# Two landing blocks of the experts' loads become places for split weights

## The chip, the cores and the metric

The kernel runs on one core of a Trainium2 chip. The metric is the time of one execution on the device in microseconds (us): the median of three runs.

The core has TensorE for matrix products (its matmul stream is PE in the profile, its weight loads PEld), VectorE (DVE), ScalarE (ACT), GpSimd (POOL) and SyncE (SP), whose queue issues the DMA transfers that bring the weights from device memory. Each engine works through its own instructions in order, and semaphores make an engine wait for another.

## The reference

Two layers on 256 tokens of width 1024, all in 32-bit floats. Each layer is a mixer (attention beside a gated delta rule) and a feed-forward part; the feed-forward part of the second layer is a mixture of eight experts. The change touches that part alone. Without the sorting of tokens into blocks it computes:

```python
logits = xt @ router_w + router_b                # 256 tokens x 8 experts
top_val, top_idx = lax.top_k(logits, 2)
gates = jax.nn.softmax(top_val, axis=-1)
# for each expert e and the tokens x that chose it:
gt, up = jnp.split(x @ w_gate_up[e], 2, axis=-1) # 1024 x 7168
y = (jax.nn.silu(gt) * up) @ w_down[e]           # 3584 x 1024
out[token] += gate * y
```

All eight experts are used, so all their weights (8 x 42 MB) are read once.

## The kernel before

**Splitting.** TensorE multiplies in a reduced form of 32-bit floats. To keep the accuracy each operand is taken as a high part (its rounding to that form) and a low part (the rest), and a product is the sum of three: high x high, low x high, high x low. Weights land unsplit: `load` issues a transfer of 1 MB (a unit: 128 partitions x 2048 floats) into a landing block, named raw. ScalarE rounds the unit to its high part (`wh_e`, L1058), and VectorE subtracts this from the landed unit and gets the low part (`wl_e`, L1071). When the subtraction is done, the landing block is free for another load. When TensorE is done with the unit's matmuls, the places of both parts are free.

**Blocks.** `ring` (L1507) lists the landing blocks in the order in which loads take them: seven of the eight blocks c0 to c7 that the mixer used before, and five (`NRAW`) of a pool of their own, twelve in all. Block c7 is one of three places for low parts. There are four places for high parts; only unit 0 has its high part elsewhere, in c6, so the load that takes c6 has to wait until TensorE has used unit 0.

**Order of the work.** The experts' part has 336 units. `sources` lists them: for each chunk of 512 of an expert's 3584 inner columns four units of gate and up weights, and then the two down units of the chunk before. Experts are ranked by their number of tokens. The first runs alone, then come three pairs of a full expert (up to 128 tokens) and a half one (up to 64), chunk by chunk in turn, and the last runs alone. A unit costs TensorE 12 matmuls of 512 columns for a full expert and 8 for a half one (there high and low parts of the tokens stand side by side in one operand).

`unit` calls `Weights.take(i)` ahead of the matmuls of unit i. It first sees to it that all units up to a distance ahead are cast (`hi`) and subtracted (`lo`). `pin` keeps these instructions, and the matmuls, in program order on their engines, so the two distances in `take` fix how far ScalarE and VectorE stand ahead of TensorE:

```python
self.hi(i + 4)
self.lo(i + 3)
return self.his[i], self.los[i]
```

A chunk then goes: product pg (`gu`, two units), ScalarE's SiLU of it (egt), product pu (two units), VectorE's product of both for a full expert, the down part of the chunk before (`finish`, two units, out py or pya and pyb), and the turn of the result: transposes pet for a full expert, with its split on ScalarE and VectorE (eah, eal), and products with a folding matrix, pef, for a half one (then esg and ea). Before the second chunk of the first expert stands `gates`, some 33 small VectorE instructions that work out the gates and the ranks of the experts. The rows of the experts' tokens are gathered and their results added by indirect DMAs from GpSimd (`gather`, `add_rows`).

A planner puts instructions that aren't pinned, the loads on SyncE among them, into an order of its own.

Of the kernel before, what the change touches and what calls it, by code (L numbers as in the profile page):

```python
# [12 lines left out]
F32R = mybir.dt.float32r  # L13
# [5 lines left out]
P = 128  # L19
# [5 lines left out]
NRAW = 5  # L25
# [4 lines left out]
UNIT = 2048  # L30
# [65 lines left out]
def build(ctx, tc, nc, A, out, upto=99):  # L96
# [75 lines left out]
    def block(tag, name, shape=(P, UNIT), dtype=F32):  # L172

        return cb.tile(list(shape), dtype, tag=tag, name=name)

    ring, nraw, halves = [None] * NRAW, [0], [2]

    def load(src):
        tag = ring[nraw[0] % len(ring)]
        nraw[0] += 1  # L180
        name = f"raw{nraw[0]}"
        if tag is None:
            raw = rawp.tile([P, UNIT], F32, tag="raw", name=name)
        else:
            raw = block(tag, name)
        n = UNIT // halves[0]
        for i in range(halves[0]):
            nc.sync.dma_start(raw[:, i * n:(i + 1) * n], src[:, i * n:(i + 1) * n])
        halves[0] = 1
        return raw  # L190
# [843 lines left out]
    def moe(l, ep, wp, dram):  # L1034
# [3 lines left out]
        def pin(ins):  # L1038

            return tc.keep_in_program_order(ins)  # L1040

        class Weights:
# [6 lines left out]
            def hi(self, n):  # L1049
                while len(self.his) < min(n, len(self.srcs)):  # L1050
                    i = len(self.his)
                    raw = load(source(*self.srcs[i]))
                    if self.ahead and i == 0:
                        h = block("c6", f"wh_{self.name}{i}", dtype=F32R)
                        SC.copy(h, raw)
                    else:
                        h = wp.tile([P, UNIT], F32R, tag="wh", bufs=4, name=f"wh_{self.name}{i}")
                        pin(SC.copy(h, raw))  # L1058
                    self.raws.append(raw)
                    self.his.append(h)  # L1060

            def lo(self, n):
                while len(self.los) < min(n, len(self.srcs)):
                    i = len(self.los)
                    self.hi(i + 1)
                    raw, h = self.raws[i], self.his[i]
                    if i % 3 == 0:
                        w = block("c7", f"wl_{self.name}{i}", dtype=F32R)
                    else:
                        w = wp.tile([P, UNIT], F32R, tag="wl", bufs=2, name=f"wl_{self.name}{i}")  # L1070
                    ins = V.tensor_tensor(w, raw, h, op=ALU.subtract)  # L1071
                    if i or not self.ahead:
                        pin(ins)
                    self.los.append(w)

            def take(self, i):

                self.hi(i + 4)
                self.lo(i + 3)
                return self.his[i], self.los[i]  # L1080


# [3 lines left out]
        def source(name, q, u):  # L1086
            if number[q] is None:
                number[q] = nc.values_load(who[0:1, q:q + 1], engines=[mybir.EngineType.SP], min_val=0, max_val=E - 1)
            return A[name][number[q], u]
# [413 lines left out]
    if upto >= 4:  # L1503
        with tc.tile_pool(name="wp", bufs=1) as wp, tc.tile_pool(name="over", bufs=1) as over, tc.tile_pool(name="ep", bufs=1) as ep, \
                tc.tile_pool(name="es", bufs=1) as es, \
                tc.tile_pool(name="dram", bufs=1, space=bass.MemoryType.DRAM) as dram:
            ring[:] = ["c3", "c1", "c2", "c0", "c4", "c5", "c6"] + [None] * NRAW  # L1507
            nraw[0] = 0

            over.tile([P, 384], F32, name="over")  # L1510
            moe(1, Even(ep, es), wp, dram)
# [6 lines left out]
def program(arrays, upto=99):  # L1518
    nc = bacc.Bacc("TRN2", target_bir_lowering=False, num_devices=1)
    A = {k: nc.dram_tensor(k, a.shape, mybir.dt.from_np(a.dtype), kind="ExternalInput").ap() for k, a in arrays.items()}  # L1520
    out = nc.dram_tensor("out", (1, S, D), F32, kind="ExternalOutput").ap()
    with tile.TileContext(nc, schedule_with_timeline_sim=True) as tc, ExitStack() as ctx:
        build(ctx, tc, nc, A, out, upto)
    return nc
# [46 lines left out]
```

## Time and profile before

| | us |
|---|---|
| median of three runs | 1581.25 (1579.4 to 1581.94) |
| the profiled execution | 1583.06 |
| its span, first to last instruction | 1581.3 |
| first matmul of the experts | 666.6 |
| PE busy, whole span | 1545.1 (98%) |
| PEld busy | 1330.3 (84%) |
| DVE busy | 1340.4 (85%) |
| ACT busy | 1072.6 (68%) |
| 336 subtractions for wl_e on DVE | 754.0, 2.286 each |
| 335 casts for wh_e on ACT | 634.1, 1.915 each |

The profile is of one execution. A busy share is the time in which an engine had an instruction under way; matmuls are pipelined and their ends are modelled, so PE's share says little on how many matmuls fit. Back to back, instructions overlap by about a tenth of a microsecond in the records, so the distance between starts counts. In a row of a timeline the first number is the start, the second the duration, and brackets hold the idle time of the engine ahead of the instruction and what ended it. "Waited for" is the instruction whose end released the waiting one.

### The profile page before, as it was taken

What the parts mean: (1) busy time and instruction counts of PE and PEld (TensorE: products, weight loads), DVE (VectorE), ACT (ScalarE), POOL (GpSimd) and SP (SyncE); (2) the same over time, 40 slices, a digit from 0 to 9 for tenths busy, and PEclk for the clock granted to TensorE, in tenths of its full rate; (3) what the DMA queues carried; (4) which work ended last, traced back from release to release, by engine and by line L of the source; (5) the groups of instructions that cost most, each with busy time, mean ns of one, the idle gap of its engine ahead of it and who ended that gap; (6) DMA issues with size and microseconds to landing.
All of it is one profiled execution on the core that took longest, in us unless ns stands there. A gap on an engine that the chain in (4) does not pass through costs nothing.

```text
span 1581.3 us, 23677 instructions
## 1 busy us (share of the span) xinstructions
PE 1545.1 (98%) x8946; PEld 1330.3 (84%) x8946; DVE 1340.4 (85%) x1511; ACT 1072.6 (68%) x1168; POOL 113.8 (7%) x76
## 2 busy tenths in 40 slices
PE   8999999999999999989999999999999999999997
PEld 6899999999888999878878878877877888888886
DVE  6998776655689977688889999999989999999986
ACT  6655555444575655567768887887878888878773
POOL 0420000000023010100001000010000100000100
PEclk9999999999999999999999999999999999999999
DMA  7433455555543376489999999999999999999980
GB/s 301 160 105 110 156 179 191 191 191 193 169 159 107 108 267 214 165 323 364 368 348 407 421 398 423 393 412 426 426 407 411 396 425 426 426 419 399 412 359 29
DMA packets 67514, 465.84 MB, mean 295 GB/s; under 512 B 8192, under 2 KB 8704, under 8 KB 12608
## 3 DMA queue, kind: packets, MB, share of 16 engines
q1 hardware_dynamic: 64080, 453.95, 73.2%
q0 software_dynamic: 2016, 7.08, 1.7%
q10 hardware_dynamic: 1296, 3.22, 0.6%
q8 instruction: 72, 1.18, 0.3%
q14 instruction: 50, 0.41, 0.1%
HBM read 457.41 MB, written 6.82 MB: 294 GB/s over the span
## 4 chain that ended last, share of the span: by engine, by line
PE 88%; DVE 7%; DMA 1%; ACT 1%; issue 1%; POOL 0%; DVEq 0%; ACTq 0%; SPq 0%
PE pg L1307 16%; PE pu L1307 15%; PE py L1307 12%; PE pf L333 8%; PE pd L333 4%; DVE wl_e L1071 3%; PE p_ga L333 3%; PE p_gb L333 3%; PE p_wo L333 3%; PE pef L1445 2%; PE pyb L1307 2%; PE pya L1307 2%; PE p_z L333 1%; PE p_cq L333 1%; PE p_yb L333 1%; PE p_ya L333 1%
## 5 line engine op out<-in xcount | busy, mean ns | idle before, releaser
L1071 DVE TENSOR_TENSOR wl_e<-raw,wh_e 128x2048 fp32r<-128x2048 f32 x336 | 754.0, 2286 | 10.6 <-ACT wh_e L1058 6.2
L1058 ACT CAST wh_e<-raw 128x2048 fp32r<-128x2048 f32 x335 | 634.1, 1915 | 79.3 <-PE pu L1307 24.2
L1307 PE MATMUL pg<-wh_e,hTe 128*128 128x512 f32 x728 | 250.4, 399 | 0.0
L1307 PE MATMUL pu<-wh_e,hTe 128*128 128x512 f32 x728 | 245.9, 393 | 0.0
L1307 PE MATMUL pu<-wl_e,hTe 128*128 128x512 f32 x448 | 179.9, 401 | 8.6 <-DVE wl_e L1071 7.2
L1307 PE MATMUL pg<-wl_e,hTe 128*128 128x512 f32 x448 | 176.5, 394 | 1.3 <-DVE wl_e L1071 1.3
L1307 PEld LDWEIGHTS pu<-wh_e,hTe 128*128 128x128 f32 x728 | 137.9, 189 | 27.9
L1307 PEld LDWEIGHTS pg<-wh_e,hTe 128*128 128x128 f32 x728 | 137.2, 189 | 27.2
L333 PE MATMUL pf<-hh_ffn,wh_fg 128*128 128x256 f32 x704 | 125.0, 281 | 0.0
L1307 PEld LDWEIGHTS pu<-wl_e,hTe 128*128 128x128 f32 x448 | 84.8, 189 | 38.2 <-DVE wl_e L1071 21.2
L1307 PE MATMUL py<-wl_e,eah 128*128 128x512 f32 x280 | 111.3, 398 | 2.1 <-DVE wl_e L1071 1.0
L1307 PE MATMUL py<-wh_e,eah 128*128 128x512 f32 x280 | 109.7, 392 | 0.7 <-ACT eah L1462 0.7
L1307 PE MATMUL py<-wh_e,eal 128*128 128x512 f32 x280 | 109.5, 391 | 0.0
L333 PEld LDWEIGHTS pf<-hh_ffn,wh_fg 128*128 128x128 f32 x704 | 108.2, 188 | 0.8
L1307 PEld LDWEIGHTS pg<-wl_e,hTe 128*128 128x128 f32 x448 | 84.6, 189 | 18.1 <-DVE wl_e L1071 1.7
L333 PE MATMUL pf<-hh_ffn,wl_fg 128*128 128x256 f32 x352 | 99.0, 282 | 0.0
L168 ACT CAST wh_fg<-raw 128x1024 fp32r<-128x1024 f32 x44 | 46.1, 1049 | 63.8 <-PE pf L333 37.5
L169 DVE TENSOR_TENSOR wl_fg<-raw,wh_fg 128x1024 fp32r<-128x1024 f32 x44 | 53.8, 1225 | 41.1 <-ACT wh_fg L168 41.0
L1307 PEld LDWEIGHTS py<-wl_e,eah 128*128 128x128 f32 x280 | 52.6, 188 | 20.2 <-DVE wl_e L1071 9.8
L333 PEld LDWEIGHTS pf<-hh_ffn,wl_fg 128*128 128x128 f32 x352 | 67.5, 192 | 0.0
L1307 PEld LDWEIGHTS py<-wh_e,eah 128*128 128x128 f32 x280 | 52.6, 188 | 12.7 <-ACT eah L1462 0.9
L1307 PEld LDWEIGHTS py<-wh_e,eal 128*128 128x128 f32 x280 | 52.6, 188 | 10.8 <-DVE eal L1463 0.4
(450 smaller groups left out, 3104.0 us busy)
## 6 DMA issues: line engine op xcount, KB each, us to landing
raw<-moe_w_gate_up SPq DMA_DIRECT2D x224, 1024.0 KB, 8.4
raw<-moe_w_down SPq DMA_DIRECT2D x112, 1024.0 KB, 8.6
raw<-w_in SPq DMA_DIRECT2D x43, 1024.0 KB, 4.8
raw<-ffn_w_gate_up SPq DMA_DIRECT2D x22, 1024.0 KB, 4.8
raw<-ffn_w_down SPq DMA_DIRECT2D x11, 1024.0 KB, 4.7
raw<-w_out SPq DMA_DIRECT2D x8, 1024.0 KB, 4.8
raw<-w_branch_b SPq DMA_DIRECT2D x4, 1024.0 KB, 5.0
raw<-w_branch_a SPq DMA_DIRECT2D x4, 1024.0 KB, 5.3
```

Source lines behind the costliest of these rows:

```text
L168: SC.copy(h[:, q], raw_ap[:, q])
L169: V.tensor_tensor(lo[:, q], raw_ap[:, q], h[:, q], op=ALU.subtract)
L333: T.matmul(o, lhsT, rhs, start=start, stop=stop)
L1058: pin(SC.copy(h, raw))
L1071: ins = V.tensor_tensor(w, raw, h, op=ALU.subtract)
L1307: pin(T.matmul(o, lhsT, rhs, start=start, stop=stop))
L1445: pin(T.matmul(pt_[:, i, t, :], r[:, t * P:(t + 1) * P], halves2, start=i + t == 0, stop=i + t == 4))
```

## The change

`ring` loses c4 and c5: ten landing blocks instead of twelve, and c6 moves from the seventh to the fifth place. c4 becomes a fifth place for high parts (of every fifth unit), c5 a fourth place for low parts; the even units' low parts now go to c7 and c5 in turn. `take` asks for one unit more ahead in both.

```diff
                     else:
-                        h = wp.tile([P, UNIT], F32R, tag="wh", bufs=4, name=f"wh_{self.name}{i}")
+                        if i % 5 == 4:
+                            h = block("c4", f"wh_{self.name}{i}", dtype=F32R)
+                        else:
+                            h = wp.tile([P, UNIT], F32R, tag="wh", bufs=4, name=f"wh_{self.name}{i}")
                         pin(SC.copy(h, raw))
...
-                    if i % 3 == 0:
-                        w = block("c7", f"wl_{self.name}{i}", dtype=F32R)
+                    if i % 2 == 0:
+                        w = block(("c7", "c5")[i // 2 % 2], f"wl_{self.name}{i}", dtype=F32R)
...
-                self.hi(i + 4)
-                self.lo(i + 3)
+                self.hi(i + 5)
+                self.lo(i + 4)
...
-            ring[:] = ["c3", "c1", "c2", "c0", "c4", "c5", "c6"] + [None] * NRAW
+            ring[:] = ["c3", "c1", "c2", "c0", "c6"] + [None] * NRAW
```

## Rows read from the trace of the kernel before

**Rows 1.** Sums by stretch: start:end, length, busy time (instructions), clock, DMA share, GB/s

```profile
700.00:800.00 100.00, 100.00 (x464) 82.45 (x463) 88.85 (x61) 73.18 (x51) 5.06 (x2) 1.00 0.96 364
790.00:1450.00 660.00, 650.55 (x3034) 526.28 (x3033) 615.29 (x385) 538.88 (x401) 29.32 (x12) 1.00 1.00 410
1300.00:1400.00 100.00, 99.61 (x465) 81.13 (x464) 94.00 (x55) 82.61 (x61) 0.00 (x0) 1.00 1.01 426
```

**Rows 2.** Waits of PEld, 790 to 1450: sum, times, longest

```profile
PEld pu L1307 <- DVE wl_e L1071: 16.9, 29, 1.7
PEld py L1307 <- DVE wl_e L1071: 9.8, 19, 0.7
```

**Rows 3.** Timeline of PE through one round of a pair

```profile
1263.55 0.48 PE L1307 MATMUL pg<-wh_e,hTe 128*128 128x512 f32 x1
...
1274.56 0.39 PE L1307 MATMUL pya<-wh_e,ea 128*128 128x512 f32 x1
...
1278.19 0.60 PE L1460 MATMUL pet<-ident,egt 128*128 128x128 f32 x4
1278.55 0.48 PE L1307 MATMUL pg<-wh_e,hTe 128*128 128x512 f32 x1
...
1287.31 0.50 PE L1307 MATMUL py<-wl_e,eah 128*128 128x512 f32 x1 [0.32 <-DVE wl_e L1071]
...
1292.66 1.00 PE L1445 MATMUL pef<-halves,egt 128*128 128x64 f32 x8
...
1294.36 0.48 PE L1307 MATMUL pg<-wh_e,hTe 128*128 128x512 f32 x1
```

**Rows 4.** Timeline of DVE in the same round

```profile
1274.76 0.69 DVE L1425 TENSOR_TENSOR egt<-pu,egt 128x512 f32<-128x512 f32 x1 [0.60 <-PE pu L1307]
1275.37 4.49 DVE L1071 TENSOR_TENSOR wl_e<-raw,wh_e 128x2048 fp32r<-128x2048 f32 x2
...
1289.52 4.49 DVE L1071 TENSOR_TENSOR wl_e<-raw,wh_e 128x2048 fp32r<-128x2048 f32 x2
1295.01 0.42 DVE L1448 TENSOR_TENSOR esg<-pef,esg 128x256 f32<-128x256 f32 x1 [1.01 <-ACT esg L1447]
```

**Rows 5.** PE at the ends of twenty rounds, and a group by line between

```profile
828.90 0.48 PE L1307 MATMUL pg<-wh_e,hTe 128*128 128x512 f32 x1
...
1447.55 0.48 PE L1307 MATMUL pg<-wh_e,hTe 128*128 128x512 f32 x1
...
L1291 PE MATMUL pgat<-ident,xg 128*128 128x128 f32 (+1 forms) x40 | 5.4, 257 | 0.0
```

**Rows 6.** Loads: median to landing; one issue, its landing, its cast

```profile
raw<-moe_w_gate_up SPq DMA_DIRECT2D x224, 1024.0 KB, 8.4
...
1042.66 0.33 SPq L188 DMA_DIRECT2D raw<-moe_w_gate_up  x1
raw<-moe_w_gate_up SPq DMA_DIRECT2D x1, 1024.0 KB, 13.7
1065.28 3.71 ACT L1058 CAST wh_e<-raw 128x2048 fp32r<-128x2048 f32 x2
```

**Rows 7.** The experts' start: SP, its landing, DVE, PE, and one stretch's sums

```profile
670.15 0.33 SPq L188 DMA_DIRECT2D raw<-moe_w_gate_up  x1
raw<-moe_w_gate_up SPq DMA_DIRECT2D x1, 1024.0 KB, 4.9
680.98 0.16 DVE L1202 COPY cnt<-pcn 128x8 f32<-128x8 f32 x1
...
687.44 4.49 DVE L1071 TENSOR_TENSOR wl_e<-raw,wh_e 128x2048 fp32r<-128x2048 f32 x2
679.06 0.66 PE L1460 MATMUL pet<-ident,egt 128*128 128x128 f32 x4 [0.78 <-DVE egt L1425]
...
689.78 0.80 PE L1307 MATMUL pu<-wl_e,hTe 128*128 128x512 f32 x1 [3.91 <-DVE wl_e L1071]
689.70:694.20 4.50, 4.42 (x10) 3.47 (x11) 4.50 (x5) 2.83 (x3) 0.00 (x0) 0.50 0.79 259
```

## The prediction, made before the changed kernel was run

> **What bounds the kernel now.** I read the sums by stretch first. From 790 to 1450 us, while a full and a half-filled expert alternate, TensorE is marked busy for 650.6 of 660 us, VectorE 615.3, ScalarE 538.9, and the DMA moves 410 GB/s; from 1300 to 1400 it moves 426 GB/s at the same share [rows 1]. Three resources stand within some per cent of their ends, so the busy shares decide nothing; the waits do. In the same stretch TensorE's weight loads waited for the low parts that VectorE writes (wl_e): 16.9 us in 29 waits before pu, 9.8 us in 19 before py [rows 2]. That is the only repeated wait of TensorE.
>
> One round (one chunk of 512 columns of the full expert and one of the half expert, 12 loads, 120 matmuls) shows where. The round goes from 1263.55 to 1294.36, 30.81 us [rows 3]. Its 48 matmuls of the full expert's pg and pu take 11.01 us, 0.229 each; the 16 of the half expert's down part 3.63 us (0.227 each); the transposes pet 0.36 us; pef 1.70 us. Between, from 1278.55 to 1292.66, lie 56 matmuls and a small gather product. At 0.227 they are 12.7 us, with about 0.4 for the gather product and restarts 13.1; they take 14.1. So about 1.0 us is lost, and the wait inside it is for wl_e [rows 3]. VectorE's rows say why: from 1274.76, when TensorE ends the full expert's pu and frees VectorE's product egt, VectorE has no pause until 1294.0 and makes a low part every 2.2 us (4.49 for two) [rows 4], while a half expert's unit lasts TensorE only 8 x 0.227 = 1.8 us. TensorE catches up with it there. Elsewhere in the round VectorE waits for TensorE: 0.60 us before egt, 1.01 us before esg [rows 4]. Each waits for the other once per round; how far the low parts run ahead (three units) sets the loss.
>
> **The change part by part.** The counts stay: 336 loads, casts and subtractions, the same matmuls, the same memory. My sum is in differences, so it starts from the profiled execution's own 1583.06 us (span 1581.3) and is carried over to the median, 1581.25, which is 1.8 us less.
>
> (1) *One unit further ahead* (take splits i+4 and casts i+5; fourth place for low parts, fifth for high parts). Let T be the end of the full expert's pu. Before, VectorE does after T: egt 0.6, two low parts 4.4, eal 0.6, then the first pu unit's low part 2.2: ready at T+7.8. TensorE wants it after 3.63 + 0.36 + 3.63 = T+7.6, and from there loses some 0.4 us per half unit. After, one low part has gone in front of egt, so it is ready at T+5.6, 2.0 us early; two units on it is T+10.1 against T+11.2; then the full expert's units last 12 x 0.227 = 2.7 us and VectorE gains. So no wait is left in a regular round.
> Is the new place in front of egt free? It needs TensorE to be done with the last unit but one, 2.7 us before T; 2.3 us of subtraction end at T-0.4, so egt is not delayed. The cast for it waits likewise for a high part's place; behind it on ScalarE stands the SiLU of pg, with no more delay than before. Late next is TensorE itself. VectorE needs 12 x 2.2 + 1.9 = 28.3 us per round, ScalarE 12 x 1.86 (3.71 for two [rows 6]) and some 3 us, both under 29.5.
> Sum: a round without waits is 11.01 + 3.63 + 0.36 + 12.7 + 0.1 + 1.70 = 29.5 us. Twenty rounds lie between 828.90 and 1447.55 [rows 5]: 618.65 us, 30.93 each. Twenty times 29.5, with 5.4 us of gather transposes [rows 5] and about 2.5 us (an estimate: 20 products at less than a transpose each) of gather products, is 598. That leaves 20.6 us; the first round, before 828.9, has waits of the same kind, which I put at 1.5 us. Term: -22. Bounds: 0, if the waits only change places, and -26.7, all of [rows 2]. I take -22, since the count of matmuls gives it without the waits' attribution.
> In the full experts' own stretches at both ends TensorE already runs 464 matmuls in 100 us [rows 1], 0.2155 each with short ones among them: nothing to gain.
>
> (2) *Ten landing blocks for twelve.* A load starts when VectorE has subtracted from the block's former content. The tightest load that I found was issued at 1042.66, landed 13.7 us later (1056.4), and its cast began at 1067.1, the second of the pair at 1065.28: 10.7 us in hand [rows 6]. Two blocks fewer start a load two units later, 2 x 2.55 = 5.1 us; that cast and subtraction both move one unit ahead cancels. 5.6 us remain: no cost while the DMA keeps pace. Pace: 12 x 1.0486 MB at 426 GB/s is 29.5 us, TensorE's round exactly. Against it work gathers, row additions and copies, which use the same DMA engines. From 790 to 1450 the DMA's whole room is 660 x (426-410)/426 = 24.8 us. Bounds for the twenty rounds: if all of it is lost to such traffic, only the 5.6 us in hand can be gained, which costs 16 us of term (1); if it is pauses, nothing. I take +1.5: from 1300 to 1400 loads move 426 GB/s while rounds of 30.9 us use 12.58/30.9 = 407, so there the loads run ahead and stop only at full blocks.
> By the Trainium skill's "Perfetto Trace Analysis", section "Identifying the Most-Contended Engine", DMA is judged by achieved bandwidth and the most contended resource is served first; 410 of 426 would make it the DMA, and a change that takes blocks from it would yield only that 5.6 us. That is rival B; no row here yet shows a cast waiting for a landing in the rounds.
>
> (3) *The start.* c6 holds the high part of unit 0 until TensorE has used it. It was the seventh place in the ring and becomes the fifth, so unit 4 now waits for it. The load so freed was issued at 670.15 and took 4.9 us [rows 7]: 675.0. Two casts, the SiLU, a third cast (1.9, 1.9, 0.6, 1.9) and three low parts behind them put egt at 683.5, since three low parts precede it now; pet follows at 684.3 instead of 679.06. That is 5.3 us of new waiting. In return unit 6's low part is ready before the gates' chain of small VectorE operations (680.98 to 687.44), behind which TensorE stood for 3.91 us at 689.78 [rows 7]. After that pause the granted clock was 0.50, the 1.2 GHz level, for 4.5 us [rows 7], ten matmuls at twice their time, some 2.1 us more. Old loss 6.0 + 0.8, new loss about 6.1 + 2.1 with nothing behind the gates (their chain ends at 692.8, the next low part at 695.0, wanted at 695.7). Difference +0.5 (the chains differ by some tenths); bounds -6, if the load comes sooner, and +8, if both waits stand.
>
> Sum: -22 + 1.5 + 0.5 = -20: 1563 for the profiled execution, **1561** for the median.
>
> **The rivals.** *B, the DMA becomes the bound.* For it: 410 of 426 GB/s. Against: the run-ahead between 1300 and 1400. It leaves 5.6 us of gain: 1581.25 - 5.6 = 1575.7, or up to 1570 if part of the room is pauses.
> *C, the wait changes its name.* TensorE waits no longer for VectorE but for ScalarE's casts or egt, or the places come free too late to be filled ahead. For it: a margin of only 0.4 us before egt. Against: ScalarE's 25 us of work in 29.5. Time: 1581, within 3 us.
> *D, slower: the queue of loads runs too shallow.* Place: the twenty rounds. With two requests fewer outstanding, pauses open between transfers. A landing takes 8.4 us (median) [rows 6], 8.4/2.55 = 3.3 loads outstanding; take two away and 1.3 remain. It decides as soon as the rate falls under 12.58 MB/30.93 us = 407 GB/s. At 400 a round lasts 31.45 us, +0.5 x 20 = +10: 1592; at the 364 GB/s of the stretch from 700 to 800 [rows 1], the nearest row with a lower rate, 34.6 us a round, +73: 1654. Against: at 364 it was TensorE that set the pace, and loads that land 10 us early may wait in a queue instead.
> The Trainium skill's "DMA: Bandwidth & Descriptors", section "Bandwidth", gives 341 GB/s for a transfer of 1 MB by itself; by that a round would be 36.9 us and the kernel 120 us slower, an estimate for a queue of depth one. No run here shows these loads one at a time in this stage.
>
> **How the numbers follow.** Forecast 0.58 (own range 1553 to 1570: the bounds of the start and half a round's error), B 0.18, C 0.11, D 0.13. Faster by over 0.2% (3.2 us, about what a measurement of this kernel can tell from no change): 0.58 + 0.18 = 0.76; within: 0.11; slower: 0.13. The range leaves out D, the upper edge of C and gains beyond 29 us, some 0.18 together: 1552 to 1582.
>
> **What would show it.** Step 1: rounds of 29.5 to 29.9 us, weight loads' waits for wl_e in the rounds down from 27 us to a few, VectorE pausing before egt. Step 2: landings closer to casts, and no casts waiting for loads; rows "ACT wh_e <- DMA raw" in the rounds would speak for B or D, with the rate telling them apart (426 or under 407). Step 3: a TensorE wait of 5 to 6 us before the first pet, and none behind the gates. The forecast is wrong if rounds stay at 30.9 us, or if the rounds shorten and the start costs over 8 us.

## The result

The changed kernel takes 1563.12 us (median of four, 1561.86 to 1565.89) against 1581.38 before: a ratio of 0.9887, 95% interval 0.9875 to 0.9899, or 18.3 us less. The prediction was 1561, between 1552 and 1582. The profiled execution has a span of 1560.1 us against 1581.3, so 21.2 less.

First the sums by stretch of the changed kernel (start:end, length, busy time of PE, PEld, DVE, ACT and POOL with instructions, clock, DMA share, GB/s); they answer to [rows 1]:

```profile
700.00:800.00 100.00, 100.00 (x464) 82.63 (x463) 92.71 (x70) 74.71 (x52) 5.54 (x2) 1.00 0.99 386
790.00:1430.00 640.00, 638.44 (x3042) 531.54 (x3042) 613.71 (x385) 539.93 (x402) 25.24 (x12) 1.00 1.01 416
1300.00:1400.00 100.00, 100.00 (x484) 83.90 (x483) 97.32 (x56) 86.18 (x63) 0.00 (x0) 1.00 1.01 427
```

Between 1300 and 1400 TensorE does 484 matmuls where it did 465. VectorE, the engine that TensorE waited for, does no less work and is busier (97.3 us of 100 for 94.0): it does not get faster, it pauses less. The full expert's own stretch (700 to 800) has 464 as before.

The waits of PEld in the pairs (790 to 1430, sum, times, longest), to be held against 16.9 and 9.8 us in [rows 2]:

```profile
PEld py L1310 <- DVE wl_e L1074: 0.8, 2, 0.6
PEld pgat L1294 <- DVE wl_e L1074: 0.7, 2, 0.4
```

The timeline of PE through the same round as in [rows 3], lines shifted by three:

```profile
1248.17 0.48 PE L1310 MATMUL pg<-wh_e,hTe 128*128 128x512 f32 x1
...
1259.19 0.39 PE L1310 MATMUL pya<-wh_e,ea 128*128 128x512 f32 x1
...
1262.82 0.60 PE L1463 MATMUL pet<-ident,egt 128*128 128x128 f32 x4
...
1276.49 1.00 PE L1448 MATMUL pef<-halves,egt 128*128 128x64 f32 x8
...
1278.19 0.48 PE L1310 MATMUL pg<-wh_e,hTe 128*128 128x512 f32 x1
```

It lasts 30.02 us instead of 30.81. From pet to pef, the part where the waits stood, it is 13.67 us instead of 14.47; the other parts are unchanged (11.02, 3.63, 1.70). A round without a gather takes 29.5 instead of 30.6. And VectorE in that round, to be held against [rows 4]:

```profile
1254.16 4.63 DVE L1074 TENSOR_TENSOR wl_e<-raw,wh_e 128x2048 fp32r<-128x2048 f32 x2
1259.39 0.69 DVE L1428 TENSOR_TENSOR egt<-pu,egt 128x512 f32<-128x512 f32 x1 [0.59 <-PE pu L1310]
1259.99 4.49 DVE L1074 TENSOR_TENSOR wl_e<-raw,wh_e 128x2048 fp32r<-128x2048 f32 x2
...
1278.83 0.42 DVE L1451 TENSOR_TENSOR esg<-pef,esg 128x256 f32<-128x256 f32 x1 [0.20 <-ACT esg L1450]
```

It still arrives before egt and waits 0.59 us for TensorE, so one more low part in front of egt delayed nothing. The pause before esg falls from 1.01 to 0.20 us. VectorE's work in the round is the same, so this pause is the 0.8 us by which the round is shorter.

The ends of the twenty rounds [rows 5]:

```profile
827.84 0.48 PE L1310 MATMUL pg<-wh_e,hTe 128*128 128x512 f32 x1
...
1426.76 0.48 PE L1310 MATMUL pg<-wh_e,hTe 128*128 128x512 f32 x1
```

598.9 us instead of 618.65: 19.7 of the gain. Some 2 us of it come from one round alone, the eleventh, which took 33.4 us before and takes 30.1 now: there VectorE had stood 1.75 us for pheld, a small product for a gather, and TensorE then waited for low parts. The loads [rows 6]: their median to landing over the whole execution, then one issue, its landing and its cast,

```profile
raw<-moe_w_gate_up SPq DMA_DIRECT2D x224, 1024.0 KB, 13.8
```

```profile
1274.19 0.33 SPq L188 DMA_DIRECT2D raw<-moe_w_down  x1
raw<-moe_w_down SPq DMA_DIRECT2D x1, 1024.0 KB, 20.1
1294.38 1.92 ACT L1061 CAST wh_e<-raw 128x2048 fp32r<-128x2048 f32 x1
```

and ScalarE's waits for loads between 1240 and 1430 (sum, times, longest):

```profile
ACT wh_e L1061 <- DMA raw<-moe_w_gate_up: 6.3, 13, 0.6
ACT wh_e L1061 <- DMA raw<-moe_w_down: 5.1, 10, 0.7
```

The landing comes at 1294.3 and the cast 0.1 us later. Nothing is in hand between landing and cast from the fifteenth of the twenty rounds on, yet TensorE doesn't wait: the low parts still end 1.3 to 5.8 us before their first matmul. Last the start [rows 7]: the load for c6, the low parts and egt on DVE, pet on PE, and the stretch after it:

```profile
668.71 0.33 SPq L188 DMA_DIRECT2D raw<-moe_w_gate_up  x1
676.37 4.50 DVE L1074 TENSOR_TENSOR wl_e<-raw,wh_e 128x2048 fp32r<-128x2048 f32 x2 [5.10 <-ACT wh_e L1061]
681.86 2.29 DVE L1074 TENSOR_TENSOR wl_e<-raw,wh_e 128x2048 fp32r<-128x2048 f32 x1 [0.99 <-ACT wh_e L1061]
684.07 0.68 DVE L1428 TENSOR_TENSOR egt<-pu,egt 128x512 f32<-128x512 f32 x1
684.81 1.12 PE L1463 MATMUL pet<-ident,egt 128*128 128x128 f32 x4 [8.01 <-DVE egt L1428]
```

```profile
686.00:690.50 4.50, 4.50 (x14) 3.63 (x15) 3.51 (x17) 1.83 (x2) 0.00 (x0) 0.55 0.51 213
```

VectorE waits 5.10 us for the cast of unit 4, whose load waited for c6; egt stands behind three low parts, and TensorE waits 8.01 us, then runs at a granted clock of 0.55 from 686.0 to 690.5. Behind the gates it no longer waits.

### The profile page after: what moved, and what is told of

Read it like the earlier page. It is cut to its first block, busy times and chain, and to the rows that moved or that the text cites. A ratio compares the mean times of both kernels' runs of the same rounds, so it can differ in the third digit from the quotient of the medians.

```text
span 1560.1 us, 23630 instructions
## 1 busy us (share of the span) xinstructions
PE 1528.6 (98%) x8946; PEld 1333.7 (85%) x8946; DVE 1338.4 (86%) x1511; ACT 1072.8 (69%) x1168; POOL 109.2 (7%) x76
## 4 chain that ended last, share of the span: by engine, by line
PE 92%; DVE 4%; ACT 1%; issue 1%; DMA 1%; POOL 0%; SPq 0%; DVEq 0%; ACTq 0%
PE pg L1310 17%; PE pu L1310 17%; PE py L1310 12%; PE pf L333 8%; PE pd L333 4%; PE p_ga L333 3%; PE p_gb L333 3%; PE p_wo L333 3%; PE pyb L1310 2%; PE pya L1310 2%; PE pef L1448 2%; PE p_z L333 1%; PE p_cq L333 1%; PE p_ya L333 1%; PE p_yb L333 1%; PE p_ck L333 1%
## 5 line engine op out<-in xcount | busy, mean ns | idle before, releaser
L1310 PE MATMUL pu<-wl_e,hTe 128*128 128x512 f32 x448 | 174.7, 390 | 0.0
## 6 DMA issues: line engine op xcount, KB each, us to landing
raw<-moe_w_gate_up SPq DMA_DIRECT2D x224, 1024.0 KB, 13.8
raw<-moe_w_down SPq DMA_DIRECT2D x112, 1024.0 KB, 13.9
```

The lines of the kernel that those rows point to most:

```text
L1310: pin(T.matmul(o, lhsT, rhs, start=start, stop=stop))
```

## The experiments

All ratios are to the kernel before, run on the same chip beside them. "Twenty rounds" is the time between the same two matmuls as in [rows 5], in each kernel's trace; "first ten units" is from the experts' first matmul to unit 10's.

| kernel | median us | ratio (95%) | twenty rounds | first ten units |
|---|---|---|---|---|
| before | 1581.4 to 1581.9 | 1 | 618.7 | 37.2 |
| changed | 1563.1 | 0.9887 (0.9875 to 0.9899) | 598.9 | 40.2 |
| ten blocks alone | 1589.2 | 1.0037 (1.0024 to 1.0050) | 620.5 | 42.0 |
| low parts alone | 1568.7 | 0.9916 (0.9901 to 0.9931) | 604.3 | 36.8 |
| high parts alone | 1584.8 | 1.0018 (1.0009 to 1.0028) | 617.8 | 40.9 |
| c6 last | 1555.8 | 0.9836 (0.9822 to 0.9849) | 599.4 | 32.8 |
| c6 last, eight blocks | 1561.0 | 0.9870 (0.9855 to 0.9885) | 603.5 | 33.1 |
| c6 last, unit 7's low part before the gates | 1557.4 | 0.9845 (0.9832 to 0.9859) | 600.3 | 33.1 |
| c6 last, gates later | 1558.4 | 0.9852 (0.9839 to 0.9866) | 599.8 | 30.9 |
| the last, and egt before unit 6's low part | 1557.4 | 0.9841 (0.9828 to 0.9855) | 598.9 | 29.8 |

**The blocks alone.** The kernel before with the shorter ring and nothing else:

```diff
-ring[:] = ["c3", "c1", "c2", "c0", "c4", "c5", "c6"] + [None] * NRAW
+ring[:] = ["c3", "c1", "c2", "c0", "c6"] + [None] * NRAW
```

> The kernel before with ten landing blocks alone: c4 and c5 leave the ring and hold nothing, three low and four high places and the old distances stay. Splitting theory (the gain is TensorE's vanished waits for low parts, bought by the distance): rounds of the pairs stay near 30.9 us each, since 10.7 us in hand at the tightest load less 5 are still positive; the start gets worse, since unit 4's load now waits for c6 and the gates' wait at unit 6 stays too: 5 to 9 us. Time 1586 to 1591. Rival 'blocks' (a shorter list of loads by itself makes the rounds shorter, less crowding of the DMA): rounds near 30, time near 1566. Rival 'depth' (two requests fewer slow the loads): rounds over 31.4, DMA under 407 GB/s, time over 1600.

Measured 1589.2. The rounds stay at 31.0 us each and the low parts' waits at what they were; DMA moves 413 GB/s between 830 and 1420, with a median of 8.1 us to landing. These are, of that kernel, PEld's waits and the two waits of PE at the start:

```profile
PEld pu L1307 <- DVE wl_e L1071: 16.4, 27, 1.6
PEld py L1307 <- DVE wl_e L1071: 9.3, 18, 0.7
```

```profile
685.00 1.12 PE L1460 MATMUL pet<-ident,egt 128*128 128x128 f32 x4 [6.26 <-DVE egt L1425]
...
696.18 0.79 PE L1307 MATMUL pu<-wl_e,hTe 128*128 128x512 f32 x1 [2.55 <-DVE wl_e L1071]
```

Fewer blocks by themselves bring nothing in the rounds, and do not slow the loads either: the rivals "blocks" and "depth" both fall. The start has both waits.

**Low parts alone.** c5 as a fourth place for low parts, `lo` one further; four high places, eleven blocks:

```diff
-ring[:] = ["c3", "c1", "c2", "c0", "c4", "c5", "c6"] + [None] * NRAW
+ring[:] = ["c3", "c1", "c2", "c0", "c4", "c6"] + [None] * NRAW
...
-                    if i % 3 == 0:
-                        w = block("c7", f"wl_{self.name}{i}", dtype=F32R)
+                    if i % 2 == 0:
+                        w = block(("c7", "c5")[i // 2 % 2], f"wl_{self.name}{i}", dtype=F32R)
...
-                self.lo(i + 3)
+                self.lo(i + 4)
```

> Half of the change: c5 becomes the fourth place for low parts and VectorE stands one unit further ahead, ScalarE's casts keep their four places and distance, eleven landing blocks. Splitting theory, worked out through one round: a low part now has to wait for a cast that itself waits until TensorE has left the high place one unit before, so it ends about 1.5 us after the end of pu instead of 0.4 before, egt comes 1.3 us later (nobody wants it before 3.6), and the half units' low parts are ready within some 0.3 us of when TensorE wants them: rounds of 29.6 to 30.3 us, most of the gain, time 1564 to 1572. Rival 'both places are needed': rounds 30.9, no gain, time 1581 to 1586.

Measured 1568.7, with 30.2 us per round: 14.3 of the 19.7 us of the rounds. Its waits of PEld, and VectorE around egt in the round of [rows 4]:

```profile
PEld py L1307 <- DVE wl_e L1071: 7.1, 15, 0.6
PEld pu L1307 <- DVE wl_e L1071: 0.7, 3, 0.2
```

```profile
1260.91 4.57 DVE L1071 TENSOR_TENSOR wl_e<-raw,wh_e 128x2048 fp32r<-128x2048 f32 x2 [0.57 <-ACT wh_e L1058]
1265.40 0.68 DVE L1425 TENSOR_TENSOR egt<-pu,egt 128x512 f32<-128x512 f32 x1
```

The waits before pu are all but gone, those before py remain at 0.5 us each. VectorE now waits for the cast (0.57) and has no pause before egt; that is the later low part that was worked out (it ends 1.6 us after pu). From 820 to 1440 its low parts wait 24.9 us for casts in this kernel, 5.9 in the kernel before and 2.7 in the changed one.

**High parts alone.** c4 as a fifth place for high parts, `hi` one further; three low places, eleven blocks:

```diff
-ring[:] = ["c3", "c1", "c2", "c0", "c4", "c5", "c6"] + [None] * NRAW
+ring[:] = ["c3", "c1", "c2", "c0", "c5", "c6"] + [None] * NRAW
...
+                        if i % 5 == 4:
+                            h = block("c4", f"wh_{self.name}{i}", dtype=F32R)
+                        else:
...
-                self.hi(i + 4)
+                self.hi(i + 5)
```

> The other half: c4 becomes the fifth place for high parts and the casts go one unit further ahead, VectorE keeps three places and its distance, eleven landing blocks. Splitting theory: VectorE's order is that of the kernel before, and it rarely waited for a cast there, so rounds stay at 30.7 to 31.0 us; the start may cost some us as unit 5's load now waits for c6: 1581 to 1587. Rival 'casts were the limit': rounds near 30, time near 1566.

Measured 1584.8, rounds of 30.9 us. Alone it gains nothing: the casts weren't what was late. With the low place it is worth the other 5.4 us of the rounds, since it frees VectorE from the waits for the cast (24.9 us without it, 2.7 with it). The two places are no sum of two gains, but a chain of which the low part is the end.

**c6 last in the ring.** The changed kernel, and unit 0's block is asked for by the tenth load instead of the fifth:

```diff
-ring[:] = ["c3", "c1", "c2", "c0", "c6"] + [None] * NRAW
+ring[:] = ["c3", "c1", "c2", "c0"] + [None] * NRAW + ["c6"]
```

> The changed kernel with one thing moved: c6, which holds unit 0's high part, goes to the end of the ring (tenth place), so unit 4's load is long there when the experts begin. Theory of the start: egt of the first chunk no longer stands behind casts that wait for that load; TensorE waits some 1.7 us before the first transposes instead of 8.0, stays at the high clock, and waits some 1.9 us for unit 7's low part behind the gates; rounds unchanged at 29.95 on the mean: 5 to 7 us faster than the changed kernel, 1556 to 1558. Rival: the wait at the start only moves behind the gates (as in the kernel before, 4 us and the clock's 2): within 2 us of the changed kernel, 1561 to 1565.

Measured 1555.8, 7.3 us under the changed kernel by the medians, with intervals that lie apart. The first ten units take 32.8 us for 40.2. PE's only wait there, and the stretch behind it, of this kernel:

```profile
677.76 0.66 PE L1463 MATMUL pet<-ident,egt 128*128 128x128 f32 x4 [1.55 <-DVE egt L1428]
```

```profile
679.60:683.00 3.40, 3.40 (x9) 2.63 (x9) 2.99 (x17) 0.75 (x1) 0.00 (x0) 0.52 1.03 434
```

The wait for unit 7's low part that I expected behind the gates didn't come: the clock, which I had expected to stay high, fell after 1.55 us of pause, TensorE was slower for 3.4 us, and the low part was in time. This is the version that beats both.

**Eight blocks.** The last kernel with two landing blocks fewer:

```diff
-ring[:] = ["c3", "c1", "c2", "c0"] + [None] * NRAW + ["c6"]
+ring[:] = ["c3", "c1"] + [None] * NRAW + ["c6"]
```

> The kernel with c6 last in the ring, with two landing blocks fewer again (c2 and c0 leave, eight remain); splitting unchanged. In the kernel with ten, loads land with some 14 us in hand at the first rounds and 0.1 us from the ninth round on, yet TensorE does not wait, since casts stand four units ahead. Theory (the DMA is work-conserving; blocks only set how far it may run ahead): two blocks fewer take 5 us of the early lead, the lead is spent some rounds earlier, and what the DMA lost in early pauses shows at the end: the twenty rounds grow from 599 us to between 600 and 606, time 1557 to 1563. Rival 'depth' (the rate itself falls with fewer requests): DMA under 410 GB/s in the rounds, rounds over 30.8, time over 1572.

Measured 1561.0; the twenty rounds grow by 4.1 us to 603.5. The casts' waits for loads rise, and the low parts' waits come back (ACT, then PEld, from 800 and 655 to 1440):

```profile
ACT wh_e L1061 <- DMA raw<-moe_w_gate_up: 25.1, 37, 1.8
ACT wh_e L1061 <- DMA raw<-moe_w_down: 8.5, 14, 1.2
```

```profile
PEld py L1310 <- DVE wl_e L1074: 4.6, 7, 0.7
PEld pu L1310 <- DVE wl_e L1074: 2.2, 4, 0.8
```

The rate is 420 GB/s between 830 and 1420, the same as with ten. So the number of blocks doesn't set the rate here; it sets how much is landed ahead when row additions and gathers take their part of the DMA. With ten that store is spent in the fifteenth of the twenty rounds, and that just suffices; with eight it is spent by the eighth (my expectation said the ninth for ten, a miscount), and the rounds with such traffic lengthen (31.3 and 30.4 us for 30.0 and 29.5 in the two from 1246 to 1307). Not all of the 4.1 us is the store's: the first of the twenty is 0.6 us longer with 6 us still in hand and no cast waiting for a load. There, and in the eighth, VectorE waits 1.40 us for pheld, which in the kernel with ten it doesn't.

**Three tries at the rest of the start.** Unit 7's low part ahead of the gates (`ws.lo(used[0] + 4)` before `gates()`); the gates and the first gather one chunk later; and that with VectorE's first egt ahead of unit 6's low part:

```diff
-                if not off and v == 1:
+                if not off and v == 2:
                     gates()
...
-                        todo = {1: ("get", 1), 3: ("turn", 1), 4: ("get", 2), 6: ("turn", 2)}
+                        todo = {2: ("get", 1), 3: ("turn", 1), 4: ("get", 2), 6: ("turn", 2)}
...
-                self.lo(i + 4)
+                self.lo(i + (3 if i == 3 else 4))
...
                     pin(V.tensor_tensor(g, pu_, g, op=ALU.mult))
+                    ws.lo(used[0] + 3)
```

> The kernel with c6 last, and unit 7's low part asked for ahead of the gates' small instructions instead of behind them. With c6 last, unit 7's low part ends when TensorE reaches unit 7 and the first ten units take 32.7 us from the first matmul; what is lost there is 1.5 us before the first transposes and 1.7 us at the low clock after it, which this does not touch. Theory: TensorE doesn't wait behind the gates now, so no gain: within 1.5 us of the kernel with c6 last. Rival (VectorE's backlog behind the gates still reaches TensorE): 2 us or more faster.

> The kernel with c6 last, with the gates' instructions and the first gather one chunk later (ahead of the third chunk). Theory: as before the second chunk, TensorE doesn't wait behind the gates; the first wait and the low clock after it stay: within 1.5 us of the kernel with c6 last. Rival: VectorE's backlog costs 2 us or more there.

> As the last kernel, and in the first chunk VectorE's product egt comes ahead of unit 6's low part instead of behind it. Theory: pet follows pu after 0.8 us instead of 1.9, too short for the clock to fall (in the kernel of before it stayed at 2.4 GHz after 0.8 us), so 1.1 + 1.7 us come back: 2.5 to 3 us faster than with c6 last, about 1553. Rival: the clock falls for another reason after the router's small matmuls, or the wait moves to unit 6: within 1 us.

The first changed nothing beyond the noise (1557.4), as expected. Moving the gates (1558.4) gave 1.9 us in the first ten units and lost 4.1 in the next two chunks (units 10 to 22). Of the third I expected 2.5 to 3 us, and in the first ten units it is 3.0 (29.8 us for 32.8; wait 0.85 us, clock 1.00); but the time is 1557.4, no better than with c6 last. Units 10 to 22 give it back: 37.3 us for 34.5. Two waits stand there. In the trace of the kernel with the gates moved, PE waits for a low part behind the gates, and for the rows of the first gather (xg), which this kernel and the third also fetch one chunk later (a row of a timeline, then one of PE's waits):

```profile
705.90 0.50 PE L1310 MATMUL pu<-wl_e,hTe 128*128 128x512 f32 x1 [1.21 <-DVE wl_e L1074]
```

```profile
PE pgat L1294 <- DMA xg<-xd,ri: 1.8, 1, 1.8
```

By the rows of the weight loads, which stop a little longer, these waits are 1.6 and 2.3 us of the 4.1 lost; in the third kernel they are 1.6 and 1.0 of 2.8. The gates cost VectorE 6.5 us in both places, and TensorE felt them in the later one; most of the rest is the later gather's, and no run moves the gates without the gather. My expectation counted the first wait alone and was wrong on the time.

## Why the prediction was right

The sum, term by term, in the profiled executions:

| term | predicted | measured | from |
|---|---|---|---|
| twenty rounds | -20.6 | -19.7 | 618.65 to 598.9 |
| first round | -1.5 | -2.3 | unit 40 to unit 52: 38.17 to 35.85 |
| loads late, ten blocks | +1.5 | about 0 | no wait of PE in the rounds after 1240 |
| start | +0.5 | +3.0 | first ten units: 37.2 to 40.2 |
| sum | -20 | -19.0 | |

That the sum is only 1 us off is partly luck: the start cost 2.5 us more than I had said, the late loads 1.5 and the first round 0.8 less. Of the other 2.2 us of the 21.2 between the two spans, 1.5 are not the change's. The experts' first matmul comes at 665.2 us instead of 666.6: the first mixer product p_ck starts at 11.1 us instead of 13.9 (among kernels of this study, alike in that stage, it starts anywhere up to 14.4), and the clock in the router's stage gives 1.1 us of that back. The remaining 0.7 lie in the full experts' own stretches. The medians differ by 18.3, a little under the terms.

*Step 1 held*, in cause and size. The rounds fell to the 29.5 us that counting matmuls had given, VectorE still pauses before egt, and the waits for low parts went from 26.7 to 0.8 us before the products. The experiments say that it is the low parts' distance that pays, together with the place that it needs (no run separates these two): neither the shorter ring (31.0 us per round) nor the casts' place and distance (30.9) does it. Two readings were off: VectorE's pause before esg, which I took for a wait for TensorE, is by its row one for ScalarE's esg, and the loss in the round was nearer 0.8 us than 1.0, since its part from pet to pef still takes 13.67 us without waits. I had treated the two places as one step; most of it, 14.3 of 19.7, is the low part's. Rival C falls with this.

*Step 2 held in its direction, by a hair.* The lead of the loads, 10.7 us at the tightest before, is 0.1 from the fifteenth round on; I had said 5.6 while the DMA keeps pace, and it does not quite. Two blocks fewer at the old rounds leave 7.2 us at the tightest (the blocks alone, where the lead recovers behind each dip). The rest is spent by the shorter rounds: 12.58 MB in 29.5 us are 426 GB/s, and while gathers and additions run, the DMA moves less in all at the same busy share (404 to 407 GB/s from 930 to 960, from 1000 to 1060 and from 1210 to 1240). So the sign that I had named for rivals B and D came, casts that wait for loads, with the rate at 427, which is B's side. It costs nothing because none of that traffic falls into the last rounds, where the DMA moves 427 GB/s from 1290 to 1420, just what they need, and because high and low parts stand ahead. With eight blocks B's mechanism shows, but at 4 us at most, not the 16 that I had put as its bound. Rival D falls: 13.8 us to landing instead of 8.4, at 416 GB/s instead of 410, means more loads queued, not slower ones.

*Step 3 was mis-sized.* The terms that I had written down, 8.2 us of new loss against 6.8 of old, differ by 1.4 and not by the +0.5 that I put into the sum. And the wait before pet was put at 6.1 us and is 8.01. Of the 1.9 us between, 1.28 are ScalarE's: the load of the SiLU's table lay ahead of the wait for pg in the kernel before and now lies behind the two late casts. The rest is the load's: issued 3.5 us after the first matmul as before, it took 5.7 us to land instead of 4.9, so the first cast started at 674.4, 9.2 us after the first matmul, where I had 8.4. The clock's part (0.55 from 686.0 to 690.5) and the silent gates came as said. Putting c6 last takes the whole step away and 7.3 us with it.

## What to carry to other kernels

When two engines in order wait for each other once a round, count the work that stands ready on each side at the wait, in units; one unit more ahead can be worth the whole wait, and it must reach the last link of the chain (here the low part; the high part alone was worth nothing). Ten and eight landing blocks held the same rate here; what they hold is a store against other traffic: they could be given away while loads lay landed for long, and the trace shows by how many us. Shorter rounds spend that store too, since each then asks for its loads at a higher rate. When blocks change places in a ring, look at what the early ones still hold.

## What was not expected

The granted clock fell to the 1.2 GHz level after pauses of TensorE as short as 1.55 us (0.52 from 679.60 to 683.00 with c6 last), but after a pause of 1.60 us it stayed at 1.00 in the kernel with the gates moved; after 0.78 and 0.85 us it stayed. So the length of the pause alone doesn't tell it. In the router's stage just before, with small products on PE, the two profiled executions ran at 0.59 and 0.50, worth some 1.1 us (16 gather products in 2.68 and 3.75 us).
